# Gathered rows turned by a diagonal of their scales, with the shift laid in by a product

## The chip, the cores and the metric

The kernel runs on one core of a Trainium2 chip. TensorE (PE, with its weight loads PEld), VectorE (DVE), ScalarE (ACT), GpSimd (POOL) and SyncE (SP) each work through a queue of their own in order, and wait for one another by semaphores. The metric is the device time of one execution in microseconds, the median of the runs.

## The reference

Two blocks in a row on 512 tokens of 1024 channels, all in float32. The change touches only the last layer, a mixture of experts:

```python
x = x + gate1 * y
hn = rmsnorm(x, norm2_w) * (1 + scale2) + shift2      # the input of the experts
logits = hn @ router_w                                # 8 experts
top_logits, top_idx = top_k(logits, 2)                # two for each token
gates = softmax(top_logits) on the two chosen experts
y = sum over e of gates[:, e] * ((silu(hn @ wg[e]) * (hn @ wu[e])) @ wd[e])   # 1024 -> 1408 -> 1024
x = x + gate2 * y
return rmsnorm(x, final_norm_w)
```

`rmsnorm(x)` is x times one scale for each token, times a vector over the channels. So `hn` is a row of x times a vector A over the channels, times the token's scale, plus a shift B over the channels.

## The kernel before

**Products in parts.** Every weight chunk (512 KB, mostly 128 x 1024) comes by a DMA into `raw` (eight buffers), ACT rounds it into `hi`, DVE takes `lo` = raw - hi (`wload`, L238; four buffers each for hi and lo). The other factor is parted in the same way. A product is hi x hi + hi x lo + lo x hi, in the single-pass format fp32r.

**Which tokens go where.** The experts are ranked by how many tokens chose them, and taken in the order of ranks 0, 4, 1, 5, 2, 6, 3, 7. Ranks 0 and 1 hold 192 places (a tile of 128 rows and one of 64), ranks 2 and 3 hold 160 (128 and 32), ranks 4 to 7 hold 128. `tile_of` (L1557) finds for each place of a tile its token (`ii`), that token's scale (`sc`) and its gate (`iw`). In DRAM lies `hnd`, the rows of x times A, without scale and shift. `fetch` (L1562) gathers a tile's rows into `row` by an indirect DMA from POOL's queue and then multiplies the 1024 columns by the scale: on POOL (L1573), or, for the first expert (`now=True`), one half on ACT and one on DVE (L1570, L1571).

**The input of an expert.** `inputs` (L1640) turns the gathered rows so that the channels lie on the partitions. For each half m of the channels and each tile: four transposes into one PSUM tile (L1657), four ACT copies that add the shift B and round (`eh`), four DVE steps that add the shift and take away eh (`el`). The result is `ex` for experts of two tiles and `eh` for those of one.

**An expert** (`expert`, L1766). `hidden_cols` (two tiles, 22 weight chunks) or `hidden_rows` (one tile, 24 chunks) makes the hidden layer; early in it `then` calls `prepare` and `fetch` for the next expert. The down product runs over two halves j of 512 output columns, each with six weight chunks over 11 channel tiles. After the products of j = 0, `inputs` of the next expert is written out in one go, ahead of the evictions of j = 0 and of the chunks of j = 1. Then the rows go back to `yd` by an indirect DMA that adds. The last expert's output goes through `combine`, with a scratch tile for the squares (`hw("l4")`, `l5`, `l6` by column part).

**The order on each engine** is made ahead of time by a planner: it takes instructions as they are written, those of `wload` first (`high_priority`), with costs of its own, and gives each engine a fixed queue.

**In the first expert** the rows of x are written to `yd` by eight DMAs from ACT's queue (`beside`, L1852), and its second and third weight chunks are parted only after the halves of its input (`pins`).

Of the kernel before, what the change touches and what calls it, by code (L numbers as in the profile page):

```python
# [17 lines left out]
T = 512  # L18
NT = 4
D = 1024  # L20
# [157 lines left out]
def tile_kernel(ctx, tc, I, out, dbg=None, upto=99):  # L178
# [17 lines left out]
    def M(n=512):  # L196
        return pm.tile([128, n], F, tag="m", name="m")


    def act(o, i, f, bias=None, scale=None, accum=None):  # L200
        kw = {}
        if bias is not None:
            kw["bias"] = bias
        if scale is not None:
            kw["scale"] = scale
        if accum is not None:
            kw["accum_out"] = accum
        return nc.scalar.activation(out=o, in_=i, func=f, **kw).ins  # L208

    def stt(o, a, s, b, op0, op1):  # L210
        return nc.vector.scalar_tensor_tensor(out=o, in0=a, scalar=s, in1=b, op0=op0, op1=op1).ins  # L211
# [996 lines left out]
    with ExitStack() as st:  # L1208
# [316 lines left out]
        def row(n):  # L1525
            rows_[0] += 1
            return lp.tile([128, D], F, tag=f"v{rows_[0] % 4}", name="row")[0:n, :]
# [24 lines left out]
        def weights(n, ps):  # L1552
            iw = lp.tile([n, 2], F, tag=f"iw{n}", name="iw", bufs=3)
            nc.vector.reduce_sum(out=iw[:, 0:1], in_=ps[:, 5:8], axis=AX.X)
            return iw

        def tile_of(pays, n0, n, OH, real):  # L1557
            ps = dispatch(pays, n0, n, OH)
            ii, fi, sc = slots(n, ps, real)
            return n, weights(n, ps), ii, fi, row(n), sc  # L1560

        def fetch(tiles, now=False):  # L1562

            for t_ in tiles:
                nc.gpsimd.indirect_dma_start(out=t_[4], out_offset=None, in_=hnd,
                                             in_offset=bass.IndirectOffsetOnAxis(ap=t_[2][:, 0:1], axis=0))
            for t_ in tiles:
                r, sc = t_[4], t_[5]
                if now:
                    act(r[:, 0:512], r[:, 0:512], AF.Copy, scale=sc[:, 0:1])  # L1570
                    ts(r[:, 512:1024], r[:, 512:1024], sc[:, 0:1])  # L1571
                else:
                    nc.gpsimd.tensor_tensor(out=r, in0=r, in1=sc[:, 0:1].to_broadcast([t_[0], D]), op=OP.mult)  # L1573

        def places(P, W, off=0.0):
            OH = lp.tile([128, NT, 192], BF, tag="OH", name="OH", bufs=1)
# [13 lines left out]
        for n0, n in ((0, 128), (128, 64)):  # L1590
            ii, fi, sc = slots(n, dispatch(pay[:, 0], n0, n, OH0, 0, 5), False)
            cur.append([n, None, ii, fi, row(n), sc])
        fetch(cur, True)
        with tc.issue_after(last[0]):
            numbers(1, 8)

# [32 lines left out]
    with ExitStack() as st:  # L1629
# [10 lines left out]
        def inputs(tiles):  # L1640

            n = sum(t_[0] for t_ in tiles)
            if n > 128:
                e = wk.tile([128, 8, 2, 192], R, tag="ex", name="ex").rearrange("p k a t -> p k (a t)")
                eh, el = e[:, :, 0:n], e[:, :, n:2 * n]
            else:
                e = wk.tile([128, 8, 2, 128], R, tag="eh", name="eh")
                eh, el = e[:, :, 0, :], e[:, :, 1, :]
            pins = []
            for m in range(2):  # L1650
                o = 0
                for t_ in tiles:
                    w, xg = t_[0], t_[4]
                    ps = M(4 * w)
                    for k in range(4):
                        z = 512 * m + 128 * k
                        nc.tensor.transpose(ps[:, w * k:w * k + w], xg[:, z:z + 128], ident[0:w, 0:w])  # L1657
                    for k in range(4):
                        pa = act(eh[:, 4 * m + k, o:o + w], ps[:, w * k:w * k + w], AF.Identity,
                                 bias=B[:, 4 * m + k:4 * m + k + 1])  # L1660
                    for k in range(4):
                        pd = stt(el[:, 4 * m + k, o:o + w], ps[:, w * k:w * k + w], B[:, 4 * m + k:4 * m + k + 1],
                                 eh[:, 4 * m + k, o:o + w].bitcast(F), OP.add, OP.subtract)
                    o += w
                pins.append((pa, pd))
            return (e if n > 128 else (eh, el)), pins

        def emm(ps, a, b, hi, lo, first, last):
            mm(ps, a, hi, first, False)
# [96 lines left out]
        def expert(e, tiles, out_, nxt=None, beside=None):  # L1766
            if isinstance(tiles[0], list):
                tiles, (xs, pins) = tiles[0], (tiles[1][0], None)
            else:
                xs, pins = inputs(tiles)  # L1770
            ns = [t_[0] for t_ in tiles]
            after = []

            def then():
                if nxt is not None:
                    after.append(prepare(nxt))
                    fetch(after[0])

            if len(ns) > 1:
                hs = hidden_cols(e, sum(ns), xs, pins, beside, then)  # L1780
            else:
                hs = hidden_rows(e, xs, pins, beside, then)
            yts = [row(n) for n in ns] if out_ is None else None

            for j, (c0, w) in enumerate(((0, 512), (512, 512)) if out_ is None else ((0, 512), (512, 256), (768, 256))):
                m = c0 // 512
                yp = [G(w) if n == 128 else G(w)[0:2 * n] for n in ns]
                step = 1024 // w
                for k0 in range(0, 11, step):
                    kn = min(step, 11 - k0)  # L1790
                    src = I["e_d"][bass.ds(e, 1), m, :, 512 * k0:512 * (k0 + kn)].rearrange("a p n -> (a p) n")
                    if w < 512:
                        src = src.rearrange("p (k n) -> p k n", n=512)[:, :, c0 - 512 * m:c0 - 512 * m + w]
                    hi, lo = wload(src, w * kn)
                    for r in range(kn):
                        k = k0 + r
                        z = slice(w * r, w * r + w)
                        for i, (a, b) in enumerate(hs):
                            emm(yp[i], a[:, k], b[:, k] if b is not None else None, hi[:, z], lo[:, z], k == 0, k == 10)
                if j == 0 and after:  # L1800
                    after.append(inputs(after[0]))
                for i, n in enumerate(ns):
                    p = yp[i] if n == 128 else whole(yp[i], n)
                    iw = tiles[i][1][:, 0:1]
                    g = g2[m][0:n, c0 - 512 * m:c0 - 512 * m + w]
                    if out_ is None:
                        stt(yts[i][:, c0:c0 + w], p, iw, g, OP.mult, OP.mult)
                    else:
                        y = hw("h1")[:, 0:w]
                        stt(y, p, iw, g, OP.mult, OP.mult)  # L1810
                        out_(j, c0, w, y, tiles[i])
            if out_ is None:
                for i, n in enumerate(ns):
                    nc.gpsimd.indirect_dma_start(
                        out=yd, out_offset=bass.IndirectOffsetOnAxis(ap=tiles[i][2][:, 0:1], axis=0),
                        in_=yts[i], in_offset=None, compute_op=OP.add)
            return after


# [4 lines left out]
        def combine(j, c0, w, y, tile_):  # L1824
            m, c = c0 // 512, slice(c0 % 512, c0 % 512 + w)
            yh, yl = hw("l0", dt=R)[:, 0:w], hw("l1", dt=R)[:, 0:w]
            split(yh, yl, y)
            if j == 1:
                log_exp_tables()
            if j == 0:  # L1830
                place["oh"] = hw("h2", dt=R)
                ts(place["oh"], row512, tile_[3][:, 0:1], op0=OP.is_equal)
            for t in range(NT):
                ps = M(w)
                o = place["oh"][:, 128 * t:128 * t + 128]
                mm(ps, o, yh, True, False)
                mm(ps, o, yl, False, True)
                a = acc[t, m][:, c]
                tt(a, a, ps, OP.add)
                act(hw(f"l{4 + j}")[:, 0:w], a, AF.Square, accum=fz[:, j, t:t + 1])  # L1840
                e, rs = fz[:, 3, t:t + 1], fz[:, 4, t:t + 1]
                if j == 0:
                    ts(e, fz[:, 0, t:t + 1], 1.0 / D, EPS, OP.mult, OP.add)
                elif j == 1:
                    stt(e, fz[:, 1, t:t + 1], 1.0 / D, e, OP.mult, OP.add)
                else:

                    act(rs, fz[:, 2, t:t + 1], AF.Ln, bias=e, scale=1.0 / D)
                    act(rs, rs, AF.Exp, scale=-0.5)
# [59 lines left out]
        with tc.For_i(0, nl, 1) as i:  # L1909
# [20 lines left out]
            parts(xpay[..., 5:8], xG, xp[:, :, 0])  # L1930
            ts(xpay[:, :, 1], xP, -1.0, p1[:, 0:1], OP.mult, OP.add)
            x_ = [tile_of(xpay, 0, 128, places(xP, 128), True)]
            fetch(x_, True)
            expert(e, x_, combine)
            final()

# [22 lines left out]
```

## Time and profile before

| what | value |
|---|---|
| median of 3 runs | 1756.07 us (1749.74 to 1757.24) |
| profiled execution | 1755.59 us |
| its span, first to last instruction | 1753.8 us |
| mean granted TensorE clock | 0.985 |
| PE busy | 1702.9 us (97%) |
| DVE busy | 1247.8 us (71%) |
| ACT busy | 857.6 us (49%) |
| the experts | from about 1209 us to the end |

Times are microseconds from the span's start. A row of the groups reads: line, engine, operation, tile written <- tiles read, sizes, count, then busy time, mean ns of one, and the idle time of the engine ahead of them with what ended it. Tiles carry the program's names without buffer numbers (`g` and `m` are the two kinds of PSUM tiles; `cst` holds the identity). In a timeline, neighbours of one kind are merged. A matmul's end is modelled, so neighbours overlap; the distance from start to start tells what one holds of PE.

### The profile page before, as it was taken

To read this page: it belongs to the slowest core of one execution; us is meant where nothing else is said; L and a number is where in the kernel's file an instruction comes from. 1 tells how busy PE (TensorE), PEld (TensorE's weight loads), DVE (VectorE), ACT (ScalarE), POOL (GpSimd) and SP (SyncE) were. 2 spreads that over 40 slices of the span, in tenths; PEclk is the share of its full clock that TensorE was granted. 3 is DMA by queue.
4 is the path that set the end of the run, shared out by engine and by line. 5 is a ranking of instruction groups with operands and counts; after the bars stand their busy time and mean duration, and the time that the engine had idled before them with its cause. 6 is when DMAs were issued, how large, how long until landed. Compare 5 with 4: busy or idle time off the path is not lost. (4 is left out here: it accounts for less than half of the span.)

```text
span 1753.8 us, 25198 instructions
## 1 busy us (share of the span) xinstructions
PE 1702.9 (97%) x8987; PEld 1426.5 (81%) x8987; DVE 1247.8 (71%) x2215; ACT 857.6 (49%) x1431; POOL 78.1 (4%) x90
## 2 busy tenths in 40 slices
PE   9999998999999999999999999999999999999995
PEld 7867787787788888888878888787987987978975
DVE  7887888857666766443255766655889889889887
ACT  5535346755443222232243222444667667767675
POOL 1000001000000000000010000000001102011000
PEclk9999998999999999999999999999999999999998
DMA  8434731344426777433342111104879789889885
GB/s 273 138 114 143 228 122 50 108 159 153 154 86 210 241 244 242 140 96 91 105 127 84 58 52 61 61 25 152 311 242 373 248 251 364 266 266 343 263 290 202
DMA packets 96474, 313.02 MB, mean 178 GB/s; under 512 B 10644, under 2 KB 13972, under 8 KB 96344
## 3 DMA queue, kind: packets, MB, share of 16 engines
q1 hardware_dynamic: 90760, 295.88, 50.4%
q0 software_dynamic: 3280, 11.27, 2.8%
q10 hardware_dynamic: 2304, 4.20, 0.6%
q8 instruction: 73, 1.20, 0.3%
q14 instruction: 57, 0.47, 0.1%
HBM read 298.99 MB, written 12.32 MB: 178 GB/s over the span
## 5 line engine op out<-in xcount | busy, mean ns | idle before, releaser
L208 ACT ACTIVATE hi<-raw 128x1024 fp32r<-128x1024 f32 (+3 forms) x473 | 475.5, 1008 | 543.4 <-PE g L222 439.3
L219 DVE TENSOR_TENSOR lo<-raw,hi 128x1024 fp32r<-128x1024 f32 (+3 forms) x473 | 547.7, 1169 | 254.0 <-ACT hi L208 246.0
L222 PE MATMUL g<-xh,hi 128*128 128x512 f32 (+1 forms) x912 | 356.4, 393 | 5.0 <-ACT xh L208 5.0
L222 PE MATMUL g<-xl,hi 128*128 128x512 f32 (+1 forms) x912 | 358.1, 393 | 1.3 <-DVE xl L211 1.2
L222 PE MATMUL g<-xh,lo 128*128 128x512 f32 (+1 forms) x912 | 357.7, 393 | 0.0
L222 PEld LDWEIGHTS g<-xh,hi 128*128 128x128 f32 x912 | 173.5, 191 | 41.5 <-ACT xh L208 5.9
L222 PEld LDWEIGHTS g<-xl,hi 128*128 128x128 f32 x912 | 174.3, 191 | 36.8 <-DVE xl L211 2.8
L222 PEld LDWEIGHTS g<-xh,lo 128*128 128x128 f32 x912 | 174.4, 191 | 33.6 <-issue 1.1
L222 PE MATMUL g<-ex,hi 128*128 128x384 f32 (+1 forms) x704 | 197.1, 359 | 4.3 <-DVE ex L211 4.3
L222 PE MATMUL g<-ex,lo 128*128 128x192 f32 (+1 forms) x704 | 173.7, 247 | 1.7 <-DVE lo L219 1.6
L222 PE MATMUL g<-hi,th 128*128 128x512 f32 (+2 forms) x462 | 148.3, 384 | 0.3 <-ACT th L208 0.2
L388 DVE SCALAR_TENSOR_TENSOR ar<-ar,one,crow 128x1024 f32<-128x1024 f32 x96 | 122.0, 1283 | 24.7 <-DMA ar<-in_ada_dram 22.3
L222 PEld LDWEIGHTS g<-ex,lo 128*128 128x128 f32 x704 | 137.2, 195 | 2.7 <-DVE lo L219 2.6
L222 PEld LDWEIGHTS g<-ex,hi 128*128 128x128 f32 x704 | 135.0, 192 | 5.0 <-DVE ex L211 4.8
L222 PE MATMUL g<-hi,eh 128*128 128x512 f32 (+1 forms) x384 | 112.9, 373 | 0.0
L222 PE MATMUL g<-lo,th 128*128 128x512 f32 (+2 forms) x275 | 104.9, 382 | 0.0
L222 PEld LDWEIGHTS g<-hi,th 128*128 128x128 f32 (+1 forms) x462 | 83.1, 183 | 19.7 <-ACT th L208 1.3
L222 PEld LDWEIGHTS g<-hi,eh 128*128 128x128 f32 x384 | 70.8, 188 | 10.1
L222 PE MATMUL g<-lo,eh 128*128 128x512 f32 (+1 forms) x192 | 71.8, 374 | 4.0 <-DVE lo L219 4.0
L222 PE MATMUL g<-fh,hi 128*128 128x512 f32 (+1 forms) x198 | 73.1, 369 | 0.0
L222 PE MATMUL g<-fl,hi 128*128 128x512 f32 (+1 forms) x198 | 72.7, 367 | 0.0
L222 PE MATMUL g<-fh,lo 128*128 128x512 f32 (+1 forms) x198 | 72.7, 367 | 0.0
(473 smaller groups left out, 2516.3 us busy)
## 6 DMA issues: line engine op xcount, KB each, us to landing
ar<-in_ada_dram SPq DMA_DIRECT2D x96, 512.0 KB, 4.4
raw<-in_e_w_dram SPq DMA_DIRECT2D x88, 512.0 KB, 5.1
raw<-in_e_d_dram SPq DMA_DIRECT2D x79, 512.0 KB, 4.9
raw<-in_e_a_dram SPq DMA_DIRECT2D x64, 512.0 KB, 4.7
raw<-in_f_gu_dram SPq DMA_DIRECT2D x44, 512.0 KB, 3.6
raw<-in_e_b_dram SPq DMA_DIRECT2D x32, 384.0 KB, 7.5
raw<-in_w_in_dram SPq DMA_DIRECT2D x22, 512.0 KB, 3.5
raw<-in_f_d_dram SPq DMA_DIRECT2D x16, 512.0 KB, 3.5
```

The lines of the kernel that those rows point to most:

```text
L208: return nc.scalar.activation(out=o, in_=i, func=f, **kw).ins
L219: return nc.vector.tensor_tensor(out=o, in0=a, in1=b, op=op).ins
L222: nc.tensor.matmul(o, l, r, start=start, stop=stop)
L388: nc.vector.scalar_tensor_tensor(out=raw, in0=raw, scalar=pace["one"], in1=crow, op0=OP.mult, op1=OP.mult, accum_out=mods[:, l, i, j:j + 1])
```

## The change

The scales leave the gathered rows. For each tile a diagonal matrix is made (`diagonal`: the identity times the scales, on DVE), and the turn becomes a plain product of the gathered rows with that diagonal in place of a transpose with the identity. The shift is laid into the PSUM tile first, by a product of the identity with the shift repeated over the tile's columns. ACT then copies, and DVE subtracts, all four channel tiles of a half at once. `inputs` becomes a generator of pieces, one for each half and tile: the next expert's pieces are taken one by one during j = 1, each after the load of a down chunk and ahead of that chunk's products. The square's scratch is one tile, since `l5` and `l6` now hold the diagonals.

```diff
@@ tile_of, fetch
+        diag = {"i": 0}
+
+        def diagonal(n0, n, sc):
+
+            if n0 == 0:
+                diag["i"] = 1 - diag["i"]
+                diag["t"] = hp.tile([128, T], F, tag=("l5", "l6")[diag["i"]], name="dgs")
+            d = diag["t"][0:n, n0:n0 + n]
+            ts(d, ident[0:n, 0:n], sc[:, 0:1])
+            return d
+
         def tile_of(pays, n0, n, OH, real):
             ps = dispatch(pays, n0, n, OH)
             ii, fi, sc = slots(n, ps, real)
-            return n, weights(n, ps), ii, fi, row(n), sc
-
-        def fetch(tiles, now=False):
+            return n, weights(n, ps), ii, fi, row(n), diagonal(n0, n, sc)
+
+        def fetch(tiles):
 
             for t_ in tiles:
                 nc.gpsimd.indirect_dma_start(out=t_[4], out_offset=None, in_=hnd,
                                              in_offset=bass.IndirectOffsetOnAxis(ap=t_[2][:, 0:1], axis=0))
-            for t_ in tiles:
-                r, sc = t_[4], t_[5]
-                if now:
-                    act(r[:, 0:512], r[:, 0:512], AF.Copy, scale=sc[:, 0:1])
-                    ts(r[:, 512:1024], r[:, 512:1024], sc[:, 0:1])
-                else:
-                    nc.gpsimd.tensor_tensor(out=r, in0=r, in1=sc[:, 0:1].to_broadcast([t_[0], D]), op=OP.mult)
@@ the first expert
-        fetch(cur, True)
+        fetch(cur)
+        for c, n0 in zip(cur, (0, 128)):
+            c[5] = diagonal(n0, c[0], c[5])
@@ inputs
             for m in range(2):
-                o = 0
+                o, ks = 0, slice(4 * m, 4 * m + 4)
                 for t_ in tiles:
-                    w, xg = t_[0], t_[4]
+                    w, xg, d = t_[0], t_[4], t_[5]
                     ps = M(4 * w)
+                    p3 = ps.rearrange("p (k t) -> p k t", t=w)
+
+                    mm(p3, ident, B[:, ks, None].to_broadcast([128, 4, w]), True, False)
                     for k in range(4):
                         z = 512 * m + 128 * k
-                        nc.tensor.transpose(ps[:, w * k:w * k + w], xg[:, z:z + 128], ident[0:w, 0:w])
-                    for k in range(4):
-                        pa = act(eh[:, 4 * m + k, o:o + w], ps[:, w * k:w * k + w], AF.Identity,
-                                 bias=B[:, 4 * m + k:4 * m + k + 1])
-                    for k in range(4):
-                        pd = stt(el[:, 4 * m + k, o:o + w], ps[:, w * k:w * k + w], B[:, 4 * m + k:4 * m + k + 1],
-                                 eh[:, 4 * m + k, o:o + w].bitcast(F), OP.add, OP.subtract)
+                        mm(p3[:, k], xg[:, z:z + 128], d, False, k == 3)
+                    pa = act(eh[:, ks, o:o + w], p3, AF.Copy)
+                    pd = tt(el[:, ks, o:o + w], p3, eh[:, ks, o:o + w].bitcast(F), OP.subtract)
                     o += w
-                pins.append((pa, pd))
-            return (e if n > 128 else (eh, el)), pins
+                    if (m, o) == (1, n):
+                        pins.append((pa, pd))
+                        yield (e if n > 128 else (eh, el)), pins
+                    else:
+                        if o == n:
+                            pins.append((pa, pd))
+                        yield None
@@ expert
-                xs, pins = inputs(tiles)
+                xs, pins = list(inputs(tiles))[-1]
             ns = [t_[0] for t_ in tiles]
-            after = []
+            after, ahead, xn_ = [], None, None
...
                     hi, lo = wload(src, w * kn)
+                    if j == 1 and ahead is not None:
+                        xn_ = next(ahead, xn_)
...
                 if j == 0 and after:
-                    after.append(inputs(after[0]))
+                    ahead = inputs(after[0])
...
+            if after:
+                after.append(xn_)
             return after
@@ combine
-                act(hw(f"l{4 + j}")[:, 0:w], a, AF.Square, accum=fz[:, j, t:t + 1])
+                act(hw("l4")[:, 0:w], a, AF.Square, accum=fz[:, j, t:t + 1])
```

The loop for experts with more tokens than places, which the profiled execution does not enter, calls `fetch(x_)` in place of `fetch(x_, True)`.

## Rows read from the trace of the kernel before

**Rows 1.** The page, part 1: busy time, share of span, instructions:

```profile
span 1753.8 us, 25198 instructions
...
PE 1702.9 (97%) x8987; PEld 1426.5 (81%) x8987; DVE 1247.8 (71%) x2215; ACT 857.6 (49%) x1431; POOL 78.1 (4%) x90
```

**Rows 2.** Waits of PE from 1209 us on: total us, times, longest:

```profile
PE g L222 <- DVE lo L219: 5.6, 5, 1.3
PE g L222 <- DVE ex L211: 4.3, 3, 1.5
```

**Rows 3.** Groups of ACT, 1222 to 1700 us: busy, mean ns, idle before, releasers:

```profile
L208 ACT ACTIVATE hi<-raw 128x1024 fp32r<-128x1024 f32 x220 | 231.9, 1058 | 69.6 <-PE g L222 62.8 <-DMA raw<-in_e_a_dram 2.9 <-DMA raw<-in_e_w_dram 1.2
...
L208 ACT ACTIVATE ex<-m,mods 128x128 fp32r<-128x128 f32 x28 | 8.4, 366 | 0.0
```

**Rows 4.** Groups of DVE, 1222 to 1700 us, same columns:

```profile
L219 DVE TENSOR_TENSOR lo<-raw,hi 128x1024 fp32r<-128x1024 f32 x219 | 265.3, 1228 | 45.7 <-ACT hi L208 44.6
...
L211 DVE SCALAR_TENSOR_TENSOR ex<-m,mods,ex 128x128 fp32r<-128x128 f32 x28 | 8.4, 344 | 0.0
...
L219 DVE TENSOR_TENSOR th<-m,th 128x512 fp32r<-128x512 f32 x7 | 4.8, 683 | 0.0
```

**Rows 5.** Timeline of PE at 1145 us: start, us, what:

```profile
1145.14 1.02 PE L222 MATMUL m<-w,onesk 128*128 128x512 f32 x2
1145.60 0.79 PE L222 MATMUL g<-yl,hi 128*128 128x512 f32 x1
1146.23 0.39 PE L222 MATMUL g<-yh,lo 128*128 128x512 f32 x1
1146.46 0.40 PE L222 MATMUL g<-yh,hi 128*128 128x512 f32 x1
```

**Rows 6.** Timeline of PE at 1201 us, products:

```profile
1201.09 1.27 PE L222 MATMUL g<-q,x 128*128 128x128 f32 x10
```

**Rows 7.** Timeline of PE at 1210 us, turns by the plain identity:

```profile
1210.50 1.97 PE L1619 MATMUL g<-cst,x 128*128 128x128 f32 x16
```

**Rows 8.** Line L1573, its instructions: ns min/median/max:

```profile
L1573 POOL TENSOR_TENSOR row<-row,sc x10: 1891/2176/2601, 1238.7 to 1625.2; 128x1024 f32<-128x1024 f32 x7, 32x1024 f32<-32x1024 f32 x2, 64x1024 f32<-64x1024 f32 x1
```

**Rows 9.** Timeline, all engines, 1327 to 1334 us:

```profile
1326.91 0.96 DVE L219 TENSOR_TENSOR lo<-raw,hi 128x768 fp32r<-128x768 f32 x1
...
1327.53 2.09 POOL L1573 TENSOR_TENSOR row<-row,sc 128x1024 f32<-128x1024 f32 x1 [3.90 <-DMA row<-hnd,ii]
...
1328.41 2.02 DVE L219 TENSOR_TENSOR lo<-raw,hi 128x768 fp32r<-128x768 f32 x1
...
1330.36 1.91 DVE L215 TENSOR_SCALAR OH<-cst,P1r 128x128 bf16<-128x128 f32 x1
...
1331.35 0.52 PE L222 MATMUL g<-hi,eh 128*128 128x384 f32 x2
...
1333.19 0.44 PE L222 MATMUL g<-lo,eh 128*128 128x384 f32 x1 [1.32 <-DVE lo L219]
```

**Rows 10.** Timeline, all engines, 1352 to 1358 us:

```profile
1352.74 3.59 DVE L219 TENSOR_TENSOR lo<-raw,hi 128x1024 fp32r<-128x1024 f32 x3
...
1355.52 0.25 PE L222 MATMUL g<-ex,lo 128*128 128x192 f32 x1
1356.25 1.37 DVE L211 SCALAR_TENSOR_TENSOR ex<-m,mods,ex 128x128 fp32r<-128x128 f32 x6
...
1357.10 0.44 PE L222 MATMUL g<-ex,hi 128*128 128x384 f32 x1 [1.33 <-DVE ex L211]
```

**Rows 11.** Windows: length, busy (count) of PE, PEld, DVE, ACT, POOL, PEclk, DMA:

```profile
1488.40:1491.60 3.20, 3.20 (x15) 3.20 (x15) 3.20 (x13) 2.47 (x5) 2.43 (x2) 0.50 0.88 242
1492.00:1495.20 3.20, 3.20 (x28) 3.20 (x26) 2.11 (x5) 1.74 (x5) 0.00 (x0) 1.00 0.95 227
```

**Rows 12.** Timeline of DVE in the first expert:

```profile
1233.89 0.36 DVE L219 TENSOR_TENSOR eh<-g,eh 128x192 f32<-128x192 f32 x1 [3.09 <-DMA yd<-xrow]
...
1239.40 1.42 DVE L219 TENSOR_TENSOR eh<-eh,eh 128x192 f32<-128x192 f32 x1
```

More of the change, by code (lines that the diff above doesn't have):

```diff
@@ L1932, in tile_kernel @@
             x_ = [tile_of(xpay, 0, 128, places(xP, 128), True)]
-            fetch(x_, True)
+            fetch(x_)
             expert(e, x_, combine)
```

## The prediction

> **What bounds the kernel now.** I read the page first, then the waits of PE from 1209 us on, where the mixture of experts begins, then the groups of ACT and DVE there. PE is busy 97% of the span [rows 1]. In the experts the two engines that part the weights are held back by PE: of ACT's 69.6 us of idle time ahead of its 220 big weight copies, 62.8 end on a product of PE that frees a buffer, and only some 4 on a DMA [rows 3]; DVE then waits for ACT [rows 4]. So PE sets the end, and an edit is worth what it takes from PE's own work or from PE's waits. Those waits are few [rows 2]: 5.6 us for the low halves of weights (lo), 4.3 us for the low half of an expert's input (ex), in three waits of up to 1.5 us. All that the change can win lies there and in what follows from these waits. What it adds to PE counts in full, outside the first expert.
>
> **The change part by part.**
>
> *The multiplication on POOL goes.* Ten of 1.9 to 2.6 us [rows 8], off the chain of PE. But while the two at 1327.5 us ran, a DVE parting of 128x768 took 2.02 us in place of 0.96, and a 128x128 comparison 1.91 us; then PE, out of lo, waited 1.32 us [rows 9]. The same picture stands in three of the one-tile experts (ranks 4, 5 and 6), whose successor has two tiles: 3 x 1.32 = 4.0 us. In the first expert a 128x192 step of DVE took 1.42 us, starting 0.7 us after the first multiplication [rows 8, 12]; another of its size took 0.36 [rows 12], so 1.1 us, on DVE's way to the lo for which PE then waited. I count 5.1 us. What would be late next is the landing of the raw weights; some 4 us of ACT's waits in the whole stage end on one [rows 3], so it may give back a few tenths.
>
> *Evictions.* For a tile and half, four ACT copies of 0.366 us (1.46) become one of four times the width [rows 3], and four DVE steps of 0.344 (1.38) become one of 0.683 [rows 4]. DVE saves 0.7 us a piece, 1.4 us for each full tile. This is off PE's path, save where PE waits for ex: at 1355.5 us PE stopped because six of the old DVE steps stood behind three partings of 3.59 us [rows 10]. An expert of two tiles has 16 such steps, up to 5.5 us of DVE, in a stretch of 11 x 3 down products of 0.23 us [rows 5], 7.6 us, in which DVE also parts six weight chunks of up to 1.23 us [rows 4]. With four steps (two of 0.683, two narrower, so at most 2.7 us) DVE has at least 2.8 us less to do there, and PE reaches the need later by the shift products below. I take the three waits as gone, 4.3 us; bounds 0 and 4.3. After two of them (before 1488 and before 1614 us) the granted clock fell to 0.5, that is 1.2 GHz: 15 products in 3.2 us, where the next 3.2 us at full clock held 28 [rows 11]. PE had just stood for 1.5 us. Each such fall loses 3.2 x 13/28 = 1.5 us; 3.0 us together, which go with the waits and stay with them.
>
> *The products.* The turn by a diagonal is a plain fp32 product. Ten 128-column fp32 products took 1.27 us [rows 6], 16 turns by the plain identity 1.97 us [rows 7]: 0.127 and 0.123 each. So that edit is nothing, 0.0 to 0.3 us over all tiles. The shift product is new: 4w columns of fp32, twice per tile. At 1145.14 us two fp32 products of 512 columns and one of the single-pass kind stand between the starts 1145.14 and 1146.23, 1.09 us; a single-pass one takes 0.23 from start to start (1146.23 to 1146.46), so an fp32 one takes 0.43 [rows 5]. Seven full tiles after the first expert: 7 x 2 x 0.43 = 6.0. A 64-row tile has 256 columns, 2 x 0.215 = 0.43; two 32-row tiles 2 x 2 x 0.11 = 0.44. Sum 6.9 us, all on PE's chain. For the first expert the same product (1.3 us) needs no gathered row and fits into PE's wait for it: nothing. No row shows a moving operand that repeats one element. The bounds are one single pass of 0.23 (sum 3.7) and four of them, 0.92 (sum 14.7); I take 0.43, the row of the same kind and width.
>
> Two rules of the Trainium skill speak against these edits. "FP8 and Floating Point Precision" (TensorE Precision Notes) counts four passes through the array for a true fp32 product; "Perfetto Trace Analysis" (Transposes) wants a turn made by a transpose and not by a standard matmul. By the first the shift products would come to 14.7 us in place of 6.9. The trace agrees with neither here: an fp32 product takes less than two single passes, and both kinds of turn take the same time.
>
> *Scales and start.* Two ACT and two DVE passes over the gathered rows of the first expert go, and two copies of the identity times a scale come, as with every later tile: at most 0.34 us of DVE each, the price of a 128x128 step with two operands, hidden in the 45.7 us that DVE idles there [rows 4]. If that cover were gone it would be 12 x 0.34 = 4.1 us of DVE, and PE would wait for what part of it makes a lo late. PE waits for the scaled rows of the first expert, ACT's passes among them, and could start up to some 2 us earlier: two passes of 0.7 (DVE's 512-wide step [rows 4]) and the narrower saving of the evictions. But later in it DVE stood 3.09 us behind the DMA that writes the rows of x [rows 12], which the change doesn't touch, and PE catches up with that. I count 0; bounds 0 and 2.
>
> *Pieces between the down weights, the scratch.* The same products, later by up to three weight chunks. PE takes them in its order, and their rows have been there for long. ACT and DVE get the evictions one at a time. The last of four pieces comes ahead of the fourth of six chunks. Behind it PE has five of 11 channel tiles, 5 x 3 x 0.23 = 3.4 us, and then 16 products of the next expert on the first half of its input, 1.8 us at the pace of [rows 11]: 5.2 us, for an eviction on ACT and one on DVE (0.7 each) behind two partings of 1.23 us, 3.9 us. It fits by 1.3 us. The square's scratch is written by ACT alone before and after: nothing.
>
> Sum: 6.9 - 5.1 - 4.3 - 3.0 = -5.5 us. The profiled execution took 1755.6 us (span 1753.8 and 1.8 around it), so 1750.1. It lies 0.5 us below the median of the runs shown; I forecast 1750.1 as the median.
>
> **The rivals.**
>
> *The wait for ex stays.* The planner may again put the last DVE steps behind a third parting; that one waits for a buffer that PE frees, so having fewer steps helps little. For it: the order of [rows 10]. Against: DVE has 1.4 us less per full tile. Then 4.3 and 3.0 are not won: 1755.6 + 6.9 - 5.1 = 1757.4.
>
> *The pieces hold up the weights (slower).* Each eviction stands in ACT's queue among the weight copies and now comes when PE gets to it, between chunks. If at each of the seven transitions PE then waits for lo, it is slower once these waits pass 5.5/7 = 0.8 us each. At the 1.5 us that PE waits today [rows 2], and a clock fall of 1.5 us after every second one, 1750.1 + 10.5 + 5.2 = 1765.8. Against: PE goes on with other products now while pieces are parted, and ACT idles for PE [rows 3].
>
> *More is won.* The start gives its 2 us, and half of the shift products fall into waits that I took as gone: 1750.1 - 2 - 3.4 = 1744.7.
>
> *Plain fp32 products are slow here (slower).* The shift products take 0.92 us, four single passes: 14.7 - 6.9 = 7.8 more. The 80 turns after the first expert's take twice their 0.12: 56 full ones 6.7, 24 narrow ones some 1.5. 1750.1 + 7.8 + 8.2 = 1766.1. [rows 5, 6, 7] speak against it. The four passes are the first rule named above.
>
> **How the numbers follow.** Forecast 0.55, with its own range 1747.5 to 1753; more won 0.16; wait stays 0.17; held up 0.08; slow products 0.04. The range 1743.5 to 1759 takes in both neighbours with a us or so of a run's own spread, and leaves out the last two and the edges. A measurement of this kernel tells 0.5%, 8.8 us, from no change: the runs shown lie 7.5 us apart. Faster than 1747.3: the case of more won and the low edge of the forecast, 0.23. Slower than 1764.8: half of the held-up case and a part of the last, 0.07. Within: 0.70.
>
> **What would show it.** No POOL multiplication; DVE's 128x768 partings at 0.96 us in the fourth and later experts, and no PE wait of 1.3 us for lo in the one-tile experts. Shift products that hold PE 0.43 us from start to start; turns at 0.11. No PE wait for ex and no clock of 0.5 at the start of the two 160-row experts. An end of the first expert's eight chunks no more than 2 us earlier. I am wrong if the moving repeated element is slow, if lo or raw weights become late in the one-tile experts, or if the planner's new order moves waits elsewhere.

## The result, and the profile after

The changed kernel takes 1766.01 us (median of 9 runs, 1760.58 to 1768.31) against 1755.01 us before (9 runs, 1748.59 to 1757.24). The ratio is 1.0069, 95% interval [1.0057, 1.0080]: it is slower, by 12 us. I had forecast 1750.1 and a range up to 1759.0. The rival that I gave 4 chances in 100, slow fp32 products, said 1766.1.

The profiled execution took 1765.9 us. Part 1 of the page of the changed kernel, as in [rows 1]:

```profile
span 1764.0 us, 25312 instructions
...
PE 1720.5 (98%) x9131; PEld 1439.6 (82%) x9131; DVE 1228.2 (70%) x2153; ACT 846.2 (48%) x1357; POOL 56.8 (3%) x80
```

PE has 17.6 us more work than in [rows 1], and 144 more instructions (9131 against 8987). DVE has 19.6 us less work and ACT 11.4. So the loss is PE's own work, and the 144 can be counted. The change writes 24 shift products (12 tiles, two halves) and turns 96 times by a product where 96 transposes stood: 24 more if a product is one instruction. 24 x 2 + 96 x (2 - 1) = 144 if it is two.

The groups of PE, 1205 to 1700 us, say the same. Columns: line, engine, operation, tiles, shape of the weights, sizes and count, then busy time, mean ns, idle time before them. The changed kernel, then the turns of the kernel before:

```profile
L222 PE MATMUL m<-dgs,row 128*128 128x128 f32 x128 | 17.2, 276 | 0.3 <-DVE pay L1477 0.3
...
L222 PE MATMUL m<-mods,cst 128*128 128x512 f32 x32 | 16.5, 597 | 0.3 <-DVE sc L1549 0.3
...
L222 PE MATMUL m<-dgs,row 64*128 64x64 f32 x32 | 4.4, 278 | 0.4 <-DMA row<-hnd,ii 0.4
L222 PE MATMUL m<-dgs,row 32*128 32x32 f32 x32 | 4.3, 274 | 0.0
...
L222 PE MATMUL m<-mods,cst 128*128 128x256 f32 x8 | 2.4, 380 | 0.0
...
L222 PE MATMUL m<-mods,cst 128*128 128x128 f32 x8 | 1.5, 272 | 0.0
```

```profile
L1657 PE MATMUL m<-cst,row 128*128 128x128 f32 x64 | 10.9, 287 | 1.1 <-ACT row L208 1.1
...
L1657 PE MATMUL m<-cst,row 64*128 64x64 f32 x16 | 2.3, 280 | 0.6 <-ACT row L208 0.6
...
L1657 PE MATMUL m<-cst,row 32*128 32x32 f32 x16 | 1.7, 227 | 0.0
```

Eight full tiles, eight turns each: 64 instructions as transposes, 128 as products. Eight full tiles, two shift products each: 32 instructions. (The means are modelled ends; the timeline tells what one holds.) PE at a transition from a two-tile to a one-tile expert, in the changed kernel and then in the kernel before:

```profile
1286.42 1.02 PE L222 MATMUL m<-mods,cst 128*128 128x512 f32 x2
1287.28 1.05 PE L222 MATMUL m<-dgs,row 128*128 128x128 f32 x8
1288.09 0.48 PE L222 MATMUL g<-hi,th 128*128 128x512 f32 x1
```

```profile
1288.56 1.03 PE L1657 MATMUL m<-cst,row 128*128 128x128 f32 x8
1289.35 0.48 PE L222 MATMUL g<-hi,th 128*128 128x512 f32 x1
```

Read it from start to start, and by the count. One shift product is the pair at 1286.42, and the next instruction starts 0.86 us later. The x8 behind it are four turns, not eight: 0.81 us, 0.20 for each. Before, x8 were eight turns by transposes: 0.79 us, 0.10 for each. One full tile's input so costs PE 2 x 0.86 + 8 x 0.10 = 2.5 us more. The stage agrees: from the first expert's first down product to the next expert's first product it is 28.54 us after (1273.92 to 1302.46) and 25.86 before (1276.06 to 1301.92), 2.7 more.

What the change was to win, it won. Waits of PE, 1222 to 1770 us (where, total us, times, longest), of the changed kernel; [rows 2] is the same view of before, whose waits for lo and ex all lie in this stretch:

```profile
PE m L1769 <- DVE eh L219: 2.0, 3, 1.0
PE g L222 <- DVE ex L219: 1.1, 1, 1.1
PE g L222 <- DVE lo L219: 0.7, 1, 0.7
```

Lo is down from 5.6 to 0.7 us. The three waits for ex of before, some 4 us into the second, third and fourth two-tile experts, are gone; the one that is left is new and stands in the first expert. (The waits for eh went up, from 0.8 to 2.0 us.) The windows at the first products of the third two-tile expert (columns as in [rows 11]) show no fall of the clock:

```profile
1492.20:1495.40 3.20, 3.20 (x26) 3.18 (x25) 3.20 (x4) 2.52 (x4) 1.76 (x1) 1.00 0.63 201
1495.40:1498.60 3.20, 3.20 (x28) 3.20 (x26) 2.76 (x6) 1.76 (x5) 0.57 (x1) 1.00 0.95 191
```

It is granted in full, 1.00, with 26 and 28 products in 3.2 us, where before 15 ran at 0.50 [rows 11]; the fourth two-tile expert shows 1.00 too. In the first expert, behind the new wait, it is at 0.50 for 3.4 us (before, for 6.8 us from 1218.6 on). Its wait in PE's timeline, and the window:

```profile
1223.11 0.67 PE L222 MATMUL g<-ex,hi 128*128 128x384 f32 x1 [1.09 <-DVE ex L219]
```

```profile
1223.20:1226.60 3.40, 3.40 (x13) 3.40 (x14) 2.47 (x3) 1.54 (x3) 0.00 (x0) 0.50 1.03 413
```

The groups of DVE and of ACT, 1222 to 1700 us, show the 128x768 partings undisturbed, at 951 ns in the mean (1087 before), and the wide evictions at 682 ns on DVE, as I had taken them, and 599 on ACT, where I had taken 0.7 us. First DVE in the changed kernel, then its partings in the kernel before, then ACT in the changed kernel:

```profile
L219 DVE TENSOR_TENSOR lo<-raw,hi 128x768 fp32r<-128x768 f32 x24 | 22.6, 951 | 1.9 <-ACT hi L208 1.5
...
L219 DVE TENSOR_TENSOR eh<-m,eh 128x512 fp32r<-128x512 f32 x8 | 5.5, 682 | 1.2 <-ACT eh L208 1.2
```

```profile
L219 DVE TENSOR_TENSOR lo<-raw,hi 128x768 fp32r<-128x768 f32 x24 | 25.8, 1087 | 0.0
```

```profile
L208 ACT ACTIVATE eh<-m 128x512 fp32r<-128x512 f32 x8 | 4.8, 599 | 4.9 <-PE m L222 4.9
```

The balance by stage, from the starts of each expert's first hidden and first down product in the two traces: the hidden stages are 14.2 us shorter in sum and begin 1.0 us earlier; the down stages, in which the input of the next expert is made, are 25.7 us longer in the seven that have a next expert. That is +10.5, beside a span that grew by 10.2.

### The profile page after: what moved, and what is told of

It reads as the page before. It is cut to its first block, busy times and chain, and to the rows that moved or that the text cites. A ratio compares the mean times of both kernels' runs of the same rounds, so it can differ in the third digit from the quotient of the medians.

```text
span 1764.0 us, 25312 instructions
## 1 busy us (share of the span) xinstructions
PE 1720.5 (98%) x9131; PEld 1439.6 (82%) x9131; DVE 1228.2 (70%) x2153; ACT 846.2 (48%) x1357; POOL 56.8 (3%) x80
## 4 chain that ended last, share of the span: by engine, by line
PE 85%; DVE 5%; DMA 5%; ACT 3%; issue 2%; SPq 0%; DVEq 0%; ACTq 0%
PE g L222 74%; PE m L222 10%; DMA ar<-in_ada_dram 2%; DMA raw<-in_e_d_dram 1%; DVE lo L219 1%; DVE ar L388 1%; ACT hi L208 1%; ACT L208 1%; DMA raw<-in_e_b_dram 0%; DMA raw<-in_e_w_dram 0%; DVE SE L211 0%; DMA raw<-in_w_in_dram 0%; DVE w L219 0%; PE m L1769 0%; ACT w L208 0%
## 5 line engine op out<-in xcount | busy, mean ns | idle before, releaser
L222 PE MATMUL g<-ex,hi 128*128 128x384 f32 (+1 forms) x704 | 193.1, 354 | 1.1 <-DVE ex L219 1.1
```

The source lines that it names most:

```text
L222: nc.tensor.matmul(o, l, r, start=start, stop=stop)
```

## The experiments

Theory A: a plain fp32 product costs PE two instructions, twice what I counted, and that is the whole loss. Theory B: the pieces between the down weights, and the new order on ACT and DVE, hold up the weights. Each run was timed next to runs of the kernel before; its ratio is to those.

**No shift product.**

```diff
-                    mm(p3, ident, B[:, ks, None].to_broadcast([128, 4, w]), True, False)
...
-                        mm(p3[:, k], xg[:, z:z + 128], d, False, k == 3)
+                        mm(p3[:, k], xg[:, z:z + 128], d, True, True)
```

> The shift product is left out, so the experts' input lacks the shift; turns, order and pieces stay. Theory A (each plain fp32 product costs PE twice what I counted, and that is the whole loss): after the first expert the shift products go with 14 x 0.86 us (512 columns), 2 x 0.43 (256) and 4 x 0.22 (128), 13.8 us together: 1766.0 - 13.8 = 1752. Theory B (the pieces between the down weights and their evictions hold up the weights, the products are cheap): the pieces and waits stay, only 6.9 us of products go, and where PE waits anyway less: 1760 to 1766.

Measured 1753.92 us, ratio 1.0003 [0.9986, 1.0020], where the changed kernel has 1.0069: the shift products are worth 0.66%, 11.6 us. A fits, B does not. Its page counts 48 PE instructions less than the changed kernel, two for each of 24 products:

```profile
PE 1712.6 (98%) x9083; PEld 1439.0 (82%) x9083; DVE 1228.0 (70%) x2153; ACT 846.0 (48%) x1357; POOL 62.5 (4%) x80
```

**Turns by transposes.**

```diff
-                    mm(p3, ident, B[:, ks, None].to_broadcast([128, 4, w]), True, False)
+                    mm(p3, ident, B[:, ks, None].to_broadcast([128, 4, w]), True, True)
...
-                        mm(p3[:, k], xg[:, z:z + 128], d, False, k == 3)
+                        nc.tensor.transpose(p3[:, k], xg[:, z:z + 128], ident[0:w, 0:w])
```

> The turns are transposes with the plain identity again, one PE instruction each; the shift products are computed, and the transposes write over them, so that scale and shift are left out of the output. Order and pieces stay. Theory A: a turn by a product holds PE 0.22 us and a transpose 0.11 (128 rows), 0.09 (64) or 0.07 (32): 56 x 0.113 + 8 x 0.135 + 16 x 0.149 = 9.8 us less, 1756. Theory B: 1766, within 1.5 us, since it takes the turn by product and by transpose as equally dear.

Measured 1756.10 us, ratio 1.0011 [0.9993, 1.0029]: the turns are worth 0.58%, 10 us, which I had counted at nothing. 96 instructions less:

```profile
PE 1712.5 (98%) x9035; PEld 1430.0 (82%) x9035; DVE 1227.3 (70%) x2153; ACT 845.3 (48%) x1357; POOL 57.1 (3%) x80
```

**Both out.** The edits of the last two together: no shift product, and transposes.

> No shift product, and transposes for turns; scale and shift are left out of the output. Pieces, single wide evictions and the missing POOL multiplication stay. Theory A: 1766.0 - 13.8 - 9.8 = 1742.4, that is some 12.6 us under the kernel before, which would be what the dropped POOL work and the waits for the input were worth. Theory B: not below the kernel before by more than 2 us, since the pieces still hold up the weights: 1753 to 1759.

Measured 1740.26 us, ratio 0.9915 [0.9881, 0.9949]. This is the changed kernel without its price: PE has the 8987 instructions of before again, and of the waits little is left, 0.8 us for lo and none for ex (part 1 of the page, then the waits of PE, 1222 to 1770 us):

```profile
PE 1692.8 (97%) x8987; PEld 1418.0 (82%) x8987; DVE 1226.3 (71%) x2153; ACT 844.7 (49%) x1357; POOL 58.2 (3%) x80
```

```profile
PE m L1768 <- DVE eh L219: 1.0, 2, 0.5
PE g L222 <- DVE lo L219: 0.8, 1, 0.8
```

So the gains are real, 0.85% or 15 us (9 to 21), and the pieces, which stay in this run, take none of it back that shows. B falls. Taken out singly, the two products are worth 11.6 and 10 us; together it is 1.0069 - 0.9915, or 27 us. The 5 us between are not told from noise: this is the median of four runs, and its interval reaches 6 us either way.

**The turns alone, in the kernel before.**

```diff
-                        nc.tensor.transpose(ps[:, w * k:w * k + w], xg[:, z:z + 128], ident[0:w, 0:w])
+                        mm(ps[:, w * k:w * k + w], xg[:, z:z + 128], ident[0:w, 0:w])
```

> The kernel before, with its transposes of gathered rows made plain products with the same identity; nothing else changes, and the result is the same. Theory A: each turn after the first expert costs 0.11 to 0.15 us more on PE's chain, 9.8 us together: 0.5 to 0.6% slower than before. Theory B (the order, not the products): no difference, within 0.15%.

Measured 1763.79 us, ratio 1.0059 [1.0032, 1.0087], 10 us, with neither a diagonal nor pieces nor a shift product in the kernel. 96 instructions more than in [rows 1]:

```profile
PE 1715.2 (97%) x9083; PEld 1440.4 (82%) x9083; DVE 1250.5 (71%) x2215; ACT 859.3 (49%) x1431; POOL 83.5 (5%) x90
```

**The shift in the single-pass format.**

```diff
+        idr, Bp = wk.tile([128, 128], R, name="idr"), wk.tile([128, 2, 8], R, name="Bp")
+        act(idr, ident, AF.Copy)
+        split(Bp[:, 0], Bp[:, 1], B)
...
-                    mm(p3, ident, B[:, ks, None].to_broadcast([128, 4, w]), True, False)
+                    for i in range(2):
+                        mm(p3, idr, Bp[:, i, ks, None].to_broadcast([128, 4, w]), i == 0, False)
```

> Complete computation. The shift is parted once into a rounded half and the rest, and laid in by two products in the single-pass format with a rounded identity, in place of one plain fp32 product. Theory A: 2 x 0.23 us in place of 0.86 for 512 columns, 2 x 0.11 in place of 0.43 for 256: some 14 x 0.40 + 0.4 = 6 us less (128 columns the same), 1760. Theory B: within 1.5 us of 1766.

Measured 1762.51 us, ratio 1.0055 [1.0037, 1.0073]: 0.14% under the changed kernel, where A had 0.34% and B nothing. A's ratio, 1.0035, lies just outside the interval, B's inside it; the time decides little, and why it shows 2.5 us of the 6 stays open. PE's timeline does show the price:

```profile
1284.68 0.59 PE L222 MATMUL m<-Bp,idr 128*128 128x512 f32 x2
1285.11 1.05 PE L222 MATMUL m<-dgs,row 128*128 128x128 f32 x8
1285.92 0.48 PE L222 MATMUL g<-hi,th 128*128 128x512 f32 x1
```

Here the x2 are really two products, the two halves of the shift, and together they hold PE 0.43 us (1284.68 to 1285.11), half of the one fp32 product above. The moving operand repeats one element in both cases; so the repeated element is not what is slow.

**The input in one go.** The changed kernel without the pieces.

```diff
-                    if j == 1 and ahead is not None:
-                        xn_ = next(ahead, xn_)
...
-                    ahead = inputs(after[0])
+                    xn_ = list(inputs(after[0]))[-1]
```

> The changed kernel with the input of the next expert written out in one go after the products of j = 0, as before the change; products, diagonal and wide evictions stay. Theory A: the pieces are worth 0 to 4 us, so that it takes 1764 to 1770 us, ratio to before 1.006 to 1.009; the waits of PE for the experts' input tell which. Theory B (the pieces hold up the weights): near 1755, ratio about 1.000.

Measured 1765.30 us, ratio 1.0074 [1.0047, 1.0101]; the changed kernel has 1.0069. Spreading the pieces is worth nothing that these runs can tell: 0.9 us, and by the interval of the run between 3.9 us lost and 5.6 won. Nor do the waits for ex come back (waits of PE, 1222 to 1770 us, where no line for ex stands any more):

```profile
PE m L1769 <- DVE eh L219: 2.0, 3, 1.0
PE g L222 <- DVE lo L219: 1.1, 2, 0.7
```

So it is not the pieces that took those waits away. Left as causes are the wide evictions and the later need of PE. The run with both products out speaks for the evictions: its PE has neither new product, so needs the input no later by them, and has no wait for ex. The later need alone does not do it: the kernel before with plain turns still has 3.1 us of them, in three waits of up to 1.1. No run changes the evictions by themselves.

**The scales on ACT, in the kernel before.** This moves POOL's multiplication to ACT and to a later place, and changes nothing else.

```diff
-                else:
-                    nc.gpsimd.tensor_tensor(out=r, in0=r, in1=sc[:, 0:1].to_broadcast([t_[0], D]), op=OP.mult)
...
+        def scale_rows(tiles):
+            for t_ in tiles:
+                act(t_[4], t_[4], AF.Copy, scale=t_[5][:, 0:1])
...
                     hi, lo = wload(src, w * kn)
+                    if j == 0 and k0 == 2 and after:
+                        scale_rows(after[0])
```

> The kernel before, with one thing moved: the gathered rows are multiplied by their scales on ACT, behind the second weight chunk of the down product, in place of POOL right behind the gather. It measures the term that I put at 5.1 us (POOL holding up DVE) by itself. If the term is right: 3 to 6 us faster than before (0.2 to 0.35%), the PE waits of 1.3 us in the one-tile experts gone, the waits for the experts' input still there. If POOL was only a bystander: no difference.

Measured 1778.28 us, ratio 1.0133 [1.0096, 1.0170]: a plain miss. The group of ACT (1222 to 1700 us) points to the cause, with 25.9 of its 36.4 us of idle time put down to the landing of the rows, and the timelines of ACT and PE show one case of it:

```profile
L208 ACT ACTIVATE row<-row,sc 128x1024 f32<-128x1024 f32 x7 | 8.0, 1149 | 36.4 <-DMA row<-hnd,ii 25.9 <-issue 5.3 <-DMA raw<-in_e_w_dram 5.2
```

```profile
1325.91 0.85 ACT L208 ACTIVATE hi<-raw 128x768 fp32r<-128x768 f32 x1 [0.44 <-PE g L222]
1331.58 1.15 ACT L208 ACTIVATE row<-row,sc 128x1024 f32<-128x1024 f32 x1 [4.81 <-DMA row<-hnd,ii]
1332.63 0.83 ACT L208 ACTIVATE hi<-raw 128x768 fp32r<-128x768 f32 x1
```

```profile
1335.11 1.11 PE L1761 MATMUL m<-cst,eh 128*128 128x128 f32 x4 [4.75 <-DVE eh L219]
```

The planner put the step into the hidden stage, ahead of weight copies, at a time when the rows had not landed. ACT stood 4.81 us for them; the rounding and then the parting came late, and PE waited 4.75 us. It says nothing on POOL.

**The same, later.** One line more, which queues the step on ACT behind the rounding of that chunk:

```diff
+                        with tc.issue_after(fast["hi"]):
                             scale_rows(after[0])
```

> As the run with the scales on ACT alone, but queued on ACT behind the rounding of the second down chunk. In the earlier run ACT stood 36 us in all for gathered rows that had not landed. If that wait was its whole loss, then without it the change of POOL for ACT is worth the term of my prediction, 3 to 6 us against the kernel before (0.2 to 0.35% faster), with PE's waits for the input of the next expert still there. If ACT's 1.15 us for each tile is itself what holds up the weights, it stays at least 0.5% slower than before.

Measured 1745.86 us, ratio 0.9957 [0.9938, 0.9976]: 7.5 us faster than before (4.2 to 10.9). The group of ACT has no idle time any more, and PE (waits, 1222 to 1770 us) no wait for lo of note, but still waits for ex:

```profile
L208 ACT ACTIVATE row<-row,sc 128x1024 f32<-128x1024 f32 x7 | 8.0, 1140 | 0.0
```

```profile
PE g L222 <- DVE ex L211: 3.5, 4, 1.6
```

So the wait for the rows and the loss of the run above go together. The gain is of the size of the POOL term of the prediction, 5.1 us, but it is not that term alone. The profiled execution (1741.07 us, the fastest of the eight) has no fall of the clock at the third and fourth two-tile experts either, though shorter waits for ex of 0.4 to 0.8 us still stand there. I had counted 3.0 us for these falls beside the 5.1. The window that holds both waits at the third two-tile expert (columns as in [rows 11]) shows the clock at 1.00:

```profile
1473.60:1476.80 3.20, 2.19 (x14) 1.97 (x15) 3.20 (x8) 1.06 (x2) 0.00 (x0) 1.00 1.10 365
```

**The same, in pieces.** With the generator of pieces of the changed kernel, and the evictions, the shift and the transposes of before.

> The same, with the input of the next expert in pieces between the down weights, in the narrow evictions of before. Theory A (only the products cost): 8 to 12 us faster than before, 0.5 to 0.7%. Theory B (the pieces hold up the weights): not faster than before, and slower than the same kernel without the pieces.

Measured 1743.45 us, ratio 0.9934 [0.9909, 0.9958]. The version without pieces has 0.9957; the two intervals overlap, so the pieces' share, 0.2%, is not told from noise. With narrow evictions the waits for ex stay, pieces or not, as PE's waits show:

```profile
PE g L222 <- DVE ex L211: 3.1, 3, 1.6
...
PE m L1766 <- DVE eh L219: 2.0, 1, 2.0
```

This is the whole computation, and it beats both kernels: 0.66% under the kernel before, and by the two ratios 1.3% under the changed one. Without the pin it was slower; the trace again has ACT waiting for the landing of the rows (25.1 us by its group) and three waits of PE for eh of 4.2 to 4.5 us:

> As the run with the scales on ACT, and the input of the next expert in pieces between the down weights; shift, turns and evictions are those of before (transposes, four narrow ACT copies and four DVE steps a piece), so PE gets no new product. Theory A: the pieces cost nothing by themselves, and the waits for the input go: 10 to 13 us faster than before, about 0.6 to 0.7%. Theory B: the pieces hold up the weights, in narrow steps more than in wide ones: slower than before.

Measured 1771.01 us, ratio 1.0109 [1.0076, 1.0142].

**The rows finished on DVE.** In place of ACT's scaling and the shift in the evictions, one DVE step for each half row multiplies by the scale and adds a row of shifts; then transposes, wide evictions, pieces. The row of shifts (`b2`) is made once, by eight products.

```diff
+                for h in range(2):
+                    stt(r[:, 512 * h:512 * h + 512], r[:, 512 * h:512 * h + 512], sc[:, 0:1], b2[h][0:n], OP.mult, OP.add)
```

> A complete version without the diagonal and without the shift product: DVE multiplies the gathered rows by their scales and adds a row of shifts in one step for each half row; then transposes, one wide ACT copy and one wide DVE subtraction a piece, pieces between the down weights. Theory A: PE does what it does in the run that left out shift and scale (ratio to before 0.9915), plus at most two DVE steps of 0.7 us a tile off the chain: 10 to 14 us faster than before, 0.6 to 0.8%. Theory B: as the changed kernel, 0.5% slower than before, since the pieces stay.

Measured 1766.78 us, ratio 1.0073 [1.0046, 1.0101]. A miss of the same kind as on ACT: DVE stood 29 us for rows that had not landed, and PE waited for lo:

```profile
PE g L222 <- DVE lo L219: 12.7, 6, 4.2
PE g L222 <- DVE ex L219: 3.3, 4, 1.0
```

> As the version that finishes the gathered rows on DVE, but queued on DVE behind the parting of the second down chunk, where the rows have landed. Before, DVE stood 29 us in all for them, and PE 12.7 us for lo. Theory A: 8 to 13 us faster than before, 0.5 to 0.75%, the less because a two-tile input costs DVE four steps of 0.75 us in the down stage of a one-tile expert, where DVE has little to spare. Theory B: not faster than before.

Measured 1758.62 us, ratio 1.0029 [1.0014, 1.0044]: better, but still slower than before, a miss again. DVE (group, 1222 to 1700 us) has no idle time ahead of these steps now, but 10.4 us of work in those of full tiles alone, and the partings of the input come last in its queue (waits of PE, 1222 to 1770 us):

```profile
L211 DVE SCALAR_TENSOR_TENSOR row<-row,sc,b 128x512 f32<-128x512 f32 x14 | 10.4, 744 | 0.0
```

```profile
PE m L222 <- DVE ex L219: 10.4, 3, 3.5
```

The three long waits for ex are at the ends of the one-tile experts. What waits there is a small product of the dispatch for a later expert that writes to a PSUM tile of the kind `m`, the kind that these partings read. That DVE has too little time there is what I read from the queue; it was not tried apart.

## Why the prediction was wrong

**The step that failed** is the price of a plain fp32 product, in "The products": "so an fp32 one takes 0.43 [rows 5]", and "0.127 and 0.123 each. So that edit is nothing". I took each instruction of PE in the trace for one product of the kernel. The code says otherwise: behind [rows 5] stands a single call, `mm(ps, O128, sq)`, for each of the five heads that fill that tile late in the layer, and the trace of before has ten such instructions between 1139 and 1154 us, in pairs 0.43 to 0.53 us apart. So the x2 in [rows 5] are one product of 0.86 us. The products of [rows 6] are written 16 times and stand 32 times in the trace, so that ten of them in 1.27 us are five products. [rows 7] holds transposes, which are one instruction each. The groups of PE in the trace of before, 1139 to 1154 us and then 1195 to 1215 us, have these counts (the code writes 5 and 16 products, and 32 transposes):

```profile
L222 PE MATMUL m<-w,onesk 128*128 128x512 f32 x10 | 5.4, 620 | 0.0
```

```profile
L1619 PE MATMUL g<-cst,x 128*128 128x128 f32 x32 | 4.4, 279 | 0.0
L222 PE MATMUL g<-q,x 128*128 128x128 f32 x32 | 4.2, 280 | 0.0
```

I laid a half product beside a whole transpose and found them equal. The count of [rows 1] could have told it too, against the products that the code writes.

**The terms with the right price.** Shift: 14 x 0.86 + 2 x 0.43 + 4 x 0.22 = 13.8 us in place of 6.9; measured 11.6 by itself (0.66%, the interval of the run 0.49 to 0.83). Turns: 9.8 us in place of nothing; measured 10 in both directions, taken out of the changed kernel and put into the one before. With 5.1, 4.3 and 3.0 won as I had them, 1755.6 + 13.8 + 9.8 - 12.4 = 1766.8; measured 1766.0. That it comes out within 0.8 us is in part luck: with the measured worths, 11.6, 10 and 15, the same sum gives 1762.2, and each of the three is uncertain by some 3 to 6 us.

**The rule.** I had weighed the Trainium skill, "FP8 and Floating Point Precision" (TensorE Precision Notes), four passes for a true fp32 product, and written that the trace doesn't agree. It does: 0.86 us for 512 columns beside 0.23 for a single-pass product of that size [rows 5]. The rule of the Trainium skill, "Perfetto Trace Analysis" (Transposes), to turn by a transpose and not by a standard matmul, I had set aside for equal times; the turns take 0.20 and 0.10 us, and the rule is worth 10 us here.

**The range.** I had named four passes as the upper bound, 14.7 us, and then kept it out of the range as settled by the row. The mistake was one of reading, and the same in both rows, so that the one seemed to confirm the other.

**What was right.** POOL's contention, 5.1: the partings are undisturbed, and the run that moves the step to ACT gains 7.5 us (4.2 to 10.9), which may hold the falls of the clock too. The waits for ex and the falls of the clock behind them, 4.3 and 3.0: the three waits are gone, and the clock stays at 1.00 where it fell. That the falls "go with the waits and stay with them" is too strong, since with the scales on ACT the falls went and shorter waits stayed. All gains together, 12.4: 15 us (9 to 21) in the run with both products out. The evictions and the diagonals cost nothing that shows, though no run took either out by itself; the start moved by 1 us, inside the 0 to 2 I gave. The pieces do not hold up the weights, as I had said, and they do not help by anything the runs can tell either. The rival of the pieces gave 1765.8, as near to the measured time as the rival of the slow products: the time alone did not tell them apart, the runs did.

## What to carry to other kernels

Before a price is read from a group or a timeline, count its instructions against the calls in the code: an operation that stands twice per call costs twice what a row seems to say. A step that reads gathered rows is worth its place in the queue more than its engine: the same ten ACT steps made this kernel 1.3% slower where they stood ahead of the landing, and 0.4% faster one pin later. And where PE is the bound, work that another engine can do in its idle time should not become a product: the scale on ACT made this kernel 0.4% faster, as a diagonal it cost 10 us. The idle time has to be there: scale and shift on DVE left it 0.3% slower.

## What the runs showed of the hardware that I had not expected

A plain fp32 product is two instructions of PE and costs as much as four single passes: 0.86 us at 512 columns (0.43 for a pair of products in the single-pass format on the same sizes), 0.20 at 128, where an fp32 transpose is one instruction of 0.10.

A narrow fp32 product was not cheaper here. In the timeline of PE of the changed kernel, four turns of a full tile (128 columns each) and then four of a 32-row tile (32 columns):

```profile
1479.14 1.05 PE L222 MATMUL m<-dgs,row 128*128 128x128 f32 x8
1479.94 0.48 PE L222 MATMUL g<-hi,th 128*128 128x512 f32 x1
...
1481.72 1.07 PE L222 MATMUL m<-dgs,row 32*128 32x32 f32 x8
1482.72 0.50 PE L222 MATMUL g<-hi,th 128*128 128x512 f32 x1
```

The full ones hold PE 0.80 us (1479.14 to 1479.94), the narrow ones 1.00 (1481.72 to 1482.72).
